# Four adaLN vectors of layer 0: two re-laid on the host, two summed by column groups on TensorE

## The chip, the cores and the metric

The program runs on one core of a Trainium2 chip. The metric is the device time of one execution in microseconds (us), as the median of repeated runs. The engines are written as in the profile: PE (TensorE matmul), PEld (its weight loads), DVE (VectorE), ACT (ScalarE), POOL (GpSimd), SP (SyncE, which here issues nearly all DMAs). A die, a state or a second core play no part.

## What is computed

Two layers of a trunk: layer 0 mixes 1024 latent and 256 context tokens by windowed attention, layer 1 by gated linear attention; a squared-ReLU MLP follows each. Every sub-layer is modulated by vectors that come from `c` (latent) or `c_ctx` (context) through a map of 1024 by 6144 per layer. What the change touches is the first lines of this:

```python
c_lat = jax.nn.silu(c)
c_con = jax.nn.silu(c_ctx)
for i in range(DEPTH):
    m_lat = jnp.split((c_lat @ w_mod[i] + b_mod[i])[:, None, :], N_MOD, axis=-1)
    m_ctx = jnp.split(c_con @ w_mod[i] + b_mod[i], N_MOD, axis=-1)
    h_lat = modulate(x_lat, g_pre_mix[i], m_lat[0], m_lat[1])   # rms_norm * (1 + scale) + shift
    ...
    f_lat = channel_mlp(modulate(x_lat, g_pre_mlp[i], m_lat[3], m_lat[4]), w_mlp_in[i], w_mlp_out[i])
```

Of the six vectors of a layer, 0 and 1 are the mixer's shift and scale, 2 its gate, 3 and 4 the MLP's shift and scale, 5 its gate. All data is float32.

## The kernel before

Tokens are worked on in ten tiles of 128: tiles 0 and 1 are context, 2 to 9 latent. Matrix products with weights are made from pairs of rounded parts, high and low, in three matmuls (`mm3`, lines 226 to 231: `ah`/`al` are the parts of activations, `wqh`/`wql` and `wkvh`/`wkvl` those of the attention weights); `split` (line 212) makes the parts, one copy on ACT and one subtraction on DVE. One tile's q, k and v take 72 matmuls of 512 columns: for each of eight k-slices of the 1024 features, six for q into a two-bank PSUM tile (tag `s`, two of them) and three for k and v into a one-bank tile (tag `b`, four of them).

`first_tiles` (line 523) does tiles 0 and 1 together while the weights arrive, in an order written out by hand (`manual_schedule`, line 1598). Vectors 0 and 1 of layer 0 are made feature tile by feature tile inside it by the three functions of `mod_first` (line 364): `load(c)` fetches the 128 columns of feature tile c of both vectors for all 1024 rows of `w_mod`, as two tiles `wm` of 128 partitions by 8 by 128 numbers; `step(c)` makes 32 matmuls of 128 columns in four column groups of the PE array (two vectors by two halves of the k-slices) with the two columns of `cT` (silu of `c` and `c_ctx`) and copies the result out of PSUM on ACT; `turn(c)` transposes it and makes the columns of `G` (scale times gain) and `S` (shift) on DVE. `operand(k)` applies them to the already turned rows `xT` and splits the result into `ah` and `al`. The loop at line 552 runs, for each k: `step(k+1)`, the weights of k+1 (loads on SP, splits on ACT and DVE), `load(k+2)`, tile 0's product of slice k, `turn(k+1)` and `operand(k+1)`, tile 1's product of slice k. The engines take their instructions in this order; SP too, so a load stands behind the loads ahead of it.

Everything after `first_tiles` is put in order by the framework's planner, which simulates the engines and may move an instruction ahead of others; it also takes the memory slots. `qkv_tile` (line 569) does one tile i from 2 to 9, and calls `between(k)` behind each k-slice; `pre(i+1)` ahead of it normalises, turns (`xt`, two one-bank tiles) and modulates the next tile. The line 1605 makes the generator `mod_sums` (line 288) for vectors 2, 3 and 4 of layer 0, and line 1614 calls it 25 times over the tiles: for each vector and each of the eight row blocks of `w_mod` one load of 512 KB, and for each of the two streams (latent, context) one DVE instruction of 128 by 1024 that multiplies the block by a column of `cT` and adds it up (lines 309 and 311). After the eighth block, `mod_gate` (line 343) sums a gate over the partitions with four matmuls by ones (line 356), and `mod_columns` (line 321) does the same for a shift or scale by 16 transposes (line 332) and four reductions on DVE (line 333). Attention begins after tile 9 (`scores`, line 693: products on PE at 703 to 708, row minimum on DVE at 719). The MLP's shift and scale are read only after attention.

Of the kernel before, what the change touches and what calls it, by code (L numbers as in the profile page):

```python
# [14 lines left out]
ALU = mybir.AluOpType  # L15
# [3 lines left out]
P = 128  # L19
D = 1024  # L20
KT = D // P
# [4 lines left out]
NT = NC_T + NL_T  # L26
# [124 lines left out]
class Weights:  # L151
# [5 lines left out]
    def load(self, n=1):  # L157
        for _ in range(min(n, KT - len(self.got))):
            self.got.append(self.one(len(self.got)))
# [6 lines left out]
class Backbone:  # L166
# [121 lines left out]
    def mod_sums(self, vectors, apart=False):  # L288
# [29 lines left out]
                self.mod_gate(l, j // 3, acc) if j % 3 == 2 else self.mod_columns(l, j, acc)  # L318
        yield

    def mod_columns(self, l, j, acc):

        nc = self.nc
        which = j // 3
        out = self.const([P, 2, KT], f"{'SG'[j % 3]}{l}{which}")
        for s, a in enumerate(acc):
            col = out[:, s, :]
            for q in range(2):
                pt = self.bank("modT")
                for c in range(4):  # L330
                    kk = 4 * q + c
                    nc.tensor.transpose(pt[:, P * c : P * (c + 1)], a[:, P * kk : P * (kk + 1)], self.ident)
                nc.vector.tensor_reduce(
                    out=col[:, 4 * q : 4 * (q + 1)], in_=pt.rearrange("p (c k) -> p c k", c=4), op=ALU.add,
                    axis=mybir.AxisListType.X,
                )
            nc.vector.tensor_tensor(col, col, self.bcol[:, l, KT * j : KT * (j + 1)], op=ALU.add)
            if j % 3 == 1:
                c0 = 16 * which + 8 * l
                nc.vector.scalar_tensor_tensor(col, col, 1.0, self.cols[:, c0 : c0 + KT], ALU.add, ALU.mult)  # L340
        self.pre.setdefault((l, which), [None, None])[1 - j % 3] = out
# [22 lines left out]
    def mod_first(self):  # L364

        nc = self.nc
        G, S = (self.const([P, 2, KT], f"{n}00") for n in "GS")
        self.pre[0, 0] = G, S
        b1 = self.const([P, KT], "b1")
        nc.vector.tensor_scalar(b1, self.bcol[:, 0, 8:16], 1.0, None, ALU.add)  # L370
        w = self.t["w_mod"][0].rearrange("(k p) n -> p k n", p=P)

        def load(c):
            wm = [self.u((P, KT, P), s="wm") for _ in range(2)]
            for j in range(2):
                nc.sync.dma_start(wm[j], w[:, :, D * j + P * c : D * j + P * (c + 1)])
            return wm

        def step(c, wm):
            ps = self.ps1("mod")  # L380
            for k in range(KT):
                for j in range(2):
                    r = 64 * j + 32 * (k % 2)
                    nc.tensor.matmul(
                        ps[r : r + 32, :P], self.cT[:, 2 * k : 2 * k + 32], wm[j][:, k, :],
                        start=(k < 2), stop=(k >= KT - 2), tile_position=(0, r),
                    )
            m = self.half("mod")[:, :P]
            nc.scalar.copy(m, ps[:, :P])
            return m  # L390

        def turn(c, m):
            pc = self.ps1("modT")[:, :P]
            nc.tensor.transpose(pc, m, self.ident)
            even = self.small(4, "even")
            nc.vector.tensor_copy(even, pc.rearrange("p (j d r) -> p j d r", j=2, d=2)[:, :, 0, 0:2])
            nc.vector.scalar_tensor_tensor(
                G[:, :, c], pc[:, 96:98], b1[:, c : c + 1], even[:, 2:4], ALU.add, ALU.add
            )
            nc.vector.tensor_scalar(G[:, :, c], G[:, :, c], self.cols[:, c : c + 1], None, ALU.mult)  # L400
            nc.vector.scalar_tensor_tensor(
                S[:, :, c], pc[:, 32:34], self.bcol[:, 0, c : c + 1], even[:, 0:2], ALU.add, ALU.add
            )

        return load, step, turn
# [117 lines left out]
    def first_tiles(self, xs, h, pre):  # L523

        nc = self.nc
        load, step, turn = self.mod_first()
        self.wq, self.wkv = [], []
        wm = [load(0)]
        xT = [self.u((P, 4, 2 * P), s="xT") for _ in range(2)]
        junk = h.alloc(0)[0][0]  # L530
        xn = [self.normed(xs.pop(0), junk) for _ in range(2)]
        m = step(0, wm[0])
        for q in range(2):
            for i in range(2):
                pt = self.ps1("xt")
                for k in range(4):
                    kk = 4 * q + k
                    nc.tensor.transpose(pt[:, P * k : P * (k + 1)], xn[i][:, P * kk : P * (kk + 1)], self.ident)
                nc.scalar.copy(xT[q][:, :, P * i : P * (i + 1)], pt.rearrange("p (k t) -> p k t", k=4))
        pq, pkv = [self.ps2("q") for _ in range(2)], [self.ps1("kv") for _ in range(2)]  # L540
        G, S = self.pre[0, 0]

        def operand(k):
            t = self.half("h")[:, : 2 * P]
            nc.vector.tensor_scalar(t, xT[k // 4][:, k % 4, :], G[:, 1, k : k + 1], S[:, 1, k : k + 1], ALU.mult, ALU.add)
            self.split(t, *h.group(0, k))

        turn(0, m)
        operand(0)
        self.qkv_weights(0)  # L550
        wm.append(load(1))
        for k in range(KT):
            if k + 1 < KT:
                m = step(k + 1, wm[k + 1])
                self.qkv_weights(k + 1)
            if k + 2 < KT:
                wm.append(load(k + 2))
            self.qkv_mm(h, 0, k, pq[0], pkv[0])
            if k + 1 < KT:
                turn(k + 1, m)  # L560
                operand(k + 1)
            else:
                nxt = pre(2)
            if k == KT - 3:
                xs += [self.x_in(2), self.x_in(3)]
            self.qkv_mm(h, 1, k, pq[1], pkv[1])
        return pq, pkv, nxt
# [1011 lines left out]
    def run(self):  # L1579
        nc, t = self.nc, self.t  # L1580
# [21 lines left out]
        self.attn_consts()  # L1602
        for i in range(2):
            self.qkv_out(i, pq[i], pkv[i])
        mods = self.mod_sums([(0, 2), (0, 3), (0, 4)])
        for i in range(2, NT):
            nxt = pre(i + 1) if i + 1 < NT else None
            if i == NT - 2:
                self.kc = [self.u((P, KVH, CTX), F32R, s="kc") for _ in range(2)]
                self.qs = {}  # L1610
                for f in self.keys(0) + self.keys(1) + self.queries(self.qs, 0, 0):
                    f()
            at = (0, 2, 4, 6) if i == NT - 2 else (0, 2, 5)
            self.qkv_tile(i, h, lambda k: next(mods) if k in at else None)
            h = nxt
            if i < NT - 2:
                self.rotary(i)
# [307 lines left out]
def rope_tables():  # L1925
# [6 lines left out]
    return np.ascontiguousarray(tab.reshape(2, NL_T, P, 32).transpose(2, 0, 1, 3))  # L1932


_INS = [
    "x", "c", "ctx", "c_ctx", "w_mod", "b_mod", "g_pre_mix", "g_post_mix", "g_pre_mlp", "g_post_mlp",
    "w_mlp_in", "w_mlp_out", "attn_w_qkv", "attn_w_o", "attn_sink", "gla_w_in", "gla_w_gate_down",
# [20 lines left out]
```

## Time and profile before

| | us |
|---|---|
| runs (three) | 2611.51, 2612.23, 2617.31 |
| median | 2612.23 |
| the profiled execution | 2614.6 |
| its span, first to last instruction | 2612.5 |
| PE busy in the span | 2547.7 (98%) |
| DVE, ACT, POOL busy | 1718.6, 1259.4, 421.6 |

The span has these stretches around the change: tiles 0 and 1 with vectors 0 and 1 until about 69 us; tiles 2 to 9 with vectors 2 to 4 until about 221 us; then attention, the MLP of layer 0 and layer 1. Busy time counts overlapping instructions once, and a matmul's end is modelled, so neighbouring matmuls overlap in the timeline and their starts tell the pace. "Idle before" in brackets is the time in which the engine had nothing running before the instruction, with what ended it. PEclk is the granted clock of PE as a share of full speed; it goes between two levels, so a mean between them says which share of the stretch was at the lower one. The DMA share is the mean over 16 queues' engines, and goes over 1 where packets overlap.

### The profile page before, as it was taken

The page shows a single profiled execution, that of the slowest core. Times are in us where ns is not written, and L with a number is a line of the kernel's source. Part 1 is how long each engine was busy: PE and PEld are TensorE (multiplying, and loading weights), DVE is VectorE, ACT ScalarE, POOL GpSimd, SP SyncE. Part 2 cuts the span into 40 slices and gives each one's busy share as a digit, 9 for nine tenths or more (in the row PEclk, how much of TensorE's full clock was granted, in tenths as well). Part 3 has the DMA queues.
Part 4 walks back from the last instruction along what each step waited for, and adds up shares of the span by engine and source line. Part 5 has one row for each costly group of instructions (what it writes and reads, how often), then busy time and mean ns, then how long its engine had stood idle before and what let it go on. Part 6 is the DMA issues. An engine that isn't in the chain of part 4 may idle for free.

```text
span 2612.5 us, 36352 instructions
## 1 busy us (share of the span) xinstructions
PE 2547.7 (98%) x13523; PEld 2118.3 (81%) x13523; DVE 1718.6 (66%) x2663; ACT 1259.4 (48%) x2364; POOL 421.6 (16%) x736
## 2 busy tenths in 40 slices
PE   7998999999999999999999999999998999999998
PEld 5777888888888888788877888888887888878886
DVE  4798766756866665758768725736658656566676
ACT  3325777744544444434325635334446545445333
POOL 0354755511000000000002212212310000000001
PEclk9999999999999999999999999999999999999999
DMA  9221000222354565827245331002221554577464
GB/s 311 79 83 41 4 1 18 74 89 81 125 172 145 182 211 188 292 98 268 93 145 193 138 82 60 26 24 97 97 97 49 174 164 133 174 247 236 161 226 161
DMA packets 228129, 342.33 MB, mean 131 GB/s; under 512 B 24409, under 2 KB 122993, under 8 KB 227953
## 3 DMA queue, kind: packets, MB, share of 16 engines
q1 hardware_dynamic: 225360, 330.58, 39.0%
q0 software_dynamic: 2592, 9.44, 0.9%
q8 instruction: 106, 1.74, 0.3%
q14 instruction: 71, 0.57, 0.1%
HBM read 267.60 MB, written 72.35 MB: 130 GB/s over the span
## 4 chain that ended last, share of the span: by engine, by line
PE 84%; DVE 7%; DMA 4%; issue 2%; ACT 2%; POOL 1%; SPq 0%; DVEq 0%; POOLq 0%; ACTq 0%
PE p L229 7%; PE p L231 6%; PE p L230 6%; PE pa L230 4%; PE pa L229 4%; PE pa L231 4%; PE o L771 3%; PE pt L752 3%; PE y L231 3%; PE y L229 3%; PE y L230 3%; PE rp L230 2%; PE rp L229 2%; PE rp L231 2%; PE pc L229 2%
## 5 line engine op out<-in xcount | busy, mean ns | idle before, releaser
L230 PE MATMUL p<-ol,oh 128*128 128x512 f32 x896 | 350.0, 391 | 0.1
L231 PE MATMUL p<-oh,ol 128*128 128x512 f32 x896 | 346.2, 389 | 0.0
L229 PE MATMUL p<-oh 128*128 128x512 f32 x896 | 329.7, 392 | 6.0 <-ACT oh L213 4.8
L242 POOL TENSOR_SCALAR rs<-ss 128x1 f32<-128x1 f32 (+1 forms) x78 | 27.6, 353 | 1636.3 <-ACT later L236 1452.2
L214 DVE TENSOR_TENSOR ol<-wh,oh 128x1024 fp32r<-128x1024 f32 x128 | 153.6, 1222 | 94.9 <-ACT oh L213 94.4
L229 PEld LDWEIGHTS p<-oh 128*128 128x128 f32 x896 | 168.3, 188 | 45.3 <-ACT oh L213 6.4
L230 PEld LDWEIGHTS p<-ol,oh 128*128 128x128 f32 x896 | 168.5, 188 | 36.4 <-DVE ol L214 1.0
L231 PEld LDWEIGHTS p<-oh,ol 128*128 128x128 f32 x896 | 168.5, 188 | 35.2 <-issue 0.2
L213 ACT CAST oh<-wh 128x1024 fp32r<-128x1024 f32 x128 | 131.4, 1051 | 131.2 <-DVE wh L1114 28.8
L311 DVE SCALAR_TENSOR_TENSOR ma<-wm,cT,ma 128x1024 f32<-128x1024 f32 x112 | 149.0, 1362 | 51.5 <-DMA wm<-in_w_mod 51.5
L213 ACT CAST oh<-k 128x1024 fp32r<-128x1024 f32 x96 | 98.0, 1054 | 127.6 <-PE p L231 57.0
L214 DVE TENSOR_TENSOR wi<-wi,wi 128x512 fp32r<-128x512 f32 x176 | 116.6, 687 | 47.9 <-ACT wi L213 46.2
L944 ACT COPY s<-pa 128x512 f32<-128x512 f32 x96 | 56.1, 585 | 182.3 <-PE pa L231 178.3
L719 DVE CUSTOM_DVE_ANT_0 pr<-sc,mask,nsink 128x640 f32<-128x640 f32 (+2 forms) x144 | 108.5, 775 | 41.8 <-PE sc L708 39.9
L724 ACT ACTIVATE pr<-pr,nm 128x640 f32<-128x640 f32 (+2 forms) x160 | 118.6, 742 | 27.3 <-DVE nm L719 24.2
L214 DVE TENSOR_TENSOR ol<-k,oh 128x1024 fp32r<-128x1024 f32 x96 | 113.8, 1221 | 21.3 <-ACT oh L213 17.7
L736 POOL TENSOR_SCALAR pr<-pr,den 128x640 f32<-128x640 f32 (+2 forms) x160 | 118.1, 752 | 36.3 <-DVE den L734 16.5
L213 ACT CAST wi<-wi 128x512 fp32r<-128x512 f32 x176 | 103.6, 615 | 38.7 <-DMA hd<-h 24.1
L229 PE MATMUL y<-woh,oh 128*128 128x512 f32 x288 | 113.9, 396 | 0.0
L231 PE MATMUL y<-woh,ol 128*128 128x512 f32 x288 | 112.5, 391 | 0.9 <-DVE ol L214 0.9
L230 PE MATMUL y<-wol,oh 128*128 128x512 f32 x288 | 112.3, 390 | 0.0
L231 PE MATMUL rp<-wgh,al 128*128 128x512 f32 x288 | 112.1, 390 | 0.0
(379 smaller groups left out, 6746.0 us busy)
## 6 DMA issues: line engine op xcount, KB each, us to landing
wm<-in_w_mod SPq DMA_DIRECT2D x96, 512.0 KB, 4.6
hd<-h SPq DMA_DIRECT2D x80, 512.0 KB, 2.9
wh<-hd SPq DMA_DIRECT2D x144, 256.0 KB, 3.9
wh<-in_w_mlp_out SPq DMA_DIRECT2D x144, 256.0 KB, 4.3
wi<-in_w_mlp_in SPq DMA_DIRECT2D x64, 512.0 KB, 5.1
k<-hd SPq DMA_DIRECT2D x80, 256.0 KB, 5.3
k<-in_w_mlp_out SPq DMA_DIRECT2D x80, 256.0 KB, 5.4
x<-in_x SPq DMA_DIRECT2D x16, 512.0 KB, 3.5
```

The lines of the kernel that those rows point to most:

```text
L213: self.nc.scalar.copy(hi, src)
L214: self.nc.vector.tensor_tensor(lo, src, hi.bitcast(F32), op=ALU.subtract)
L229: mm(out, a[0], b[0], start=start, stop=False, skip_group_check=onto)
L230: mm(out, a[0], b[1], start=False, stop=False, skip_group_check=onto)
L231: mm(out, a[1], b[0], start=False, stop=stop, skip_group_check=onto)
L311: nc.vector.scalar_tensor_tensor(acc[s], raw, c, acc[s], ALU.mult, ALU.add)
L719: nc.vector.tensor_tensor_reduce(out=like(pr), in0=like(ps[e][:, off:768]), in1=mask, scale=1.0, scalar=self.nsink[:, c0 + e : c0 + e + 1] ...
L724: nc.scalar.activation(pr, pr, AF.Exp, bias=nm[:, e : e + 1], scale=-1.0, accum_out=sums[:, e : e + 1])
L736: nc.gpsimd.tensor_scalar(probs[e], probs[e], den[:, e : e + 1], 0.0, ALU.mult, ALU.add)
L752: nc.tensor.transpose(pt[:, P * j : P * (j + 1)], probs[e][:, P * kt : P * (kt + 1)], self.ident)
L771: nc.tensor.matmul(po[64 * e : 64 * (e + 1), P * i4 : P * (i4 + 1)], self.kv[tile_i // 2][:, tile_i % 2, 256 + HD * g : 256 + HD * (g + 1) ...
L944: nc.scalar.copy(s["s", j], s["pa"])
```

## The change

The first part adds an input, `first`: the host cuts columns 0 to 2047 of layer 0's `w_mod` into [feature tile, vector, partition, k-slice by column], so that each `wm` tile of `mod_first` is one contiguous block with 4 KB for each partition. What is loaded into the tile is the same.

The second part moves, for k = 0 alone, tile 0's product ahead of `step(1)` and the weights of k = 1.

The third part takes vectors 3 and 4 out of `mod_sums` and makes them in a new generator `mod_pair`: per row block two loads (the blocks of both vectors, in flight two row blocks at a time), and four matmuls with 32 columns of `cT` as weights (the first two are the streams) and 512 columns of a block, one in each column group of the array, all eight row blocks summed in one PSUM bank. One ACT copy, four transposes into a second bank, and small DVE instructions then give the columns. Its six steps are called in tiles 5 to 8; vector 2 keeps `mod_sums`, in tiles 2 to 4.

```diff
+    def mod_pair(self, l, which):
+        nc, t = self.nc, self.t
+        js = (3 * which, 3 * which + 1)
+        def load(k):
+            raw = [self.u(s="wm") for _ in js]
+            for r, j in zip(raw, js):
+                nc.sync.dma_start(r, t["w_mod"][l, P * k : P * (k + 1), D * j : D * (j + 1)])
+            return raw
+        raws = [load(0), load(1)]
+        yield
+        ps = self.ps1("mod")
+        for k in range(0, KT, 2):
+            for kk in (k, k + 1):
+                raw = raws.pop(0)
+                for b in range(4):
+                    nc.tensor.matmul(
+                        ps[32 * b : 32 * (b + 1), :], self.cT[:, 2 * kk : 2 * kk + 32],
+                        raw[b // 2][:, 512 * (b % 2) : 512 * (b % 2 + 1)],
+                        start=(kk == 0), stop=(kk == KT - 1), tile_position=(0, 32 * b),
+                    )
+            if k + 2 < KT:
+                raws += [load(k + 2), load(k + 3)]
+            else:
+                m = self.half("mod")
+                nc.scalar.copy(m, ps)
+            yield
+        pt = self.ps1("modT")
+        for c in range(4):
+            nc.tensor.transpose(pt[:, P * c : P * (c + 1)], m[:, P * c : P * (c + 1)], self.ident)
...
+            for st in range(2):
+                nc.vector.tensor_tensor(...)            # plus bias, 8 columns
+                if v == 1:
+                    nc.vector.scalar_tensor_tensor(...) # (scale + 1) * gain, 8 columns
...
-        w = self.t["w_mod"][0].rearrange("(k p) n -> p k n", p=P)
+        w = self.t["first"]
...
-                nc.sync.dma_start(wm[j], w[:, :, D * j + P * c : D * j + P * (c + 1)])
+                nc.sync.dma_start(wm[j], w[c, j].rearrange("p (k n) -> p k n", k=KT))
...
         for k in range(KT):
+            if k == 0:
+                self.qkv_mm(h, 0, k, pq[0], pkv[0])
             if k + 1 < KT:
                 m = step(k + 1, wm[k + 1])
                 self.qkv_weights(k + 1)
             if k + 2 < KT:
                 wm.append(load(k + 2))
-            self.qkv_mm(h, 0, k, pq[0], pkv[0])
+            if k > 0:
+                self.qkv_mm(h, 0, k, pq[0], pkv[0])
...
-        mods = self.mod_sums([(0, 2), (0, 3), (0, 4)])
+        mods, pair = self.mod_sums([(0, 2)]), self.mod_pair(0, 1)
...
-            at = (0, 2, 4, 6) if i == NT - 2 else (0, 2, 5)
-            self.qkv_tile(i, h, lambda k: next(mods) if k in at else None)
+            def between(k):
+                if i < 5 and k in (0, 2, 5):
+                    next(mods)
+                elif (i, k) in ((5, 5), (6, 1), (6, 5), (7, 1), (7, 5), (8, 1)):
+                    next(pair)
+            self.qkv_tile(i, h, between)
...
+def first_columns(w_mod):
+    w = w_mod[0, :, : 2 * D].reshape(KT, P, 2, KT, P)
+    return np.ascontiguousarray(w.transpose(3, 2, 1, 0, 4).reshape(KT, 2, P, KT * P))
```

## Rows read from the trace of the kernel before

**Rows 1.** Busy time by stretch, columns: length, each engine, PEclk, DMA share, GB/s.
```profile
70.00:224.00 154.00, 148.69 (x696) 121.27 (x696) 124.11 (x151) 45.51 (x87) 63.53 (x62) 0.99 0.27 86
190.00:200.00 10.00, 5.76 (x29) 5.08 (x28) 7.18 (x10) 3.29 (x8) 6.46 (x8) 0.83 0.00 0
224.00:2612.00 2388.00, 2345.05 (x12394) 1956.35 (x12392) 1561.94 (x2439) 1187.20 (x2234) 353.65 (x652) 1.00 0.40 129
```

**Rows 2.** The DMA view: packets of 20 to 45 us, then of 55 to 62.
```profile
DMA packets 10530, 8.14 MB, mean 326 GB/s; under 512 B 245, under 2 KB 9443, under 8 KB 10527
...
DMA packets 788, 2.87 MB, mean 410 GB/s; under 512 B 88, under 2 KB 88, under 8 KB 788
```

**Rows 3.** Timeline of the first stage: start, duration, engine, line, instruction, count.
```profile
10.54 1.93 PE L384 MATMUL mod<-wm,cT 128*32 128x128 f32 x30 [1.06 <-DMA wm<-in_w_mod]
...
22.72 0.48 PE L229 MATMUL q<-wqh,ah 128*128 128x512 f32 x1
...
26.11 0.27 ACT L389 COPY mod<-mod 128x128 f32<-128x128 f32 x1 [1.41 <-PE mod L384]
```

**Rows 4.** Timeline, the tail of the first stage, SP's issues among it.
```profile
45.40 4.15 SPq L479 DMA_DIRECT2D x<-in_x  x2
...
49.64 0.38 SPq L221 DMA_DIRECT2D wqr<-in_attn_w_qkv  x1
...
54.29 1.07 PE L384 MATMUL mod<-wm,cT 128*32 128x128 f32 x30 [1.54 <-DMA wm<-in_w_mod]
...
58.12 1.05 ACT L213 CAST wqh<-wqr 128x1024 fp32r<-128x1024 f32 x1 [2.35 <-DMA wqr<-in_attn_w_qkv]
...
62.08 0.66 PE L229 MATMUL q<-wqh,ah 128*128 128x512 f32 x1 [2.25 <-ACT ah L213]
...
64.03 0.75 DVE L427 TENSOR_SCALAR x<-x,rs 128x1024 f32<-128x1024 f32 x1 [1.54 <-POOL rs L243]
...
68.32 0.39 PE L230 MATMUL kv<-wkvl,ah 128*128 128x512 f32 x1
...
68.54 0.39 PE L231 MATMUL kv<-wkvh,al 128*128 128x512 f32 x1
```

**Rows 5.** Waits of SP, 0 to 70 us: total, times, longest.
```profile
SPq L479 <- DVE al L214: 8.1, 2, 6.3
```

**Rows 6.** Loads of line 221 (attention weights, 512 KB each), issue to landing.
```profile
DMA to landing us min/median/max: 5.6/7.2/8.4
```

**Rows 7.** Groups of instructions, 62 to 226 us: busy, mean ns, idle before.
```profile
L311 DVE SCALAR_TENSOR_TENSOR ma<-wm,cT,ma 128x1024 f32<-128x1024 f32 x42 | 61.0, 1498 | 7.1 <-DMA wm<-in_w_mod 7.1
...
L332 PE MATMUL modT<-ident,ma 128*128 128x128 f32 x32 | 4.3, 273 | 0.5 <-DVE ma L311 0.5
```

**Rows 8.** Timeline of PE: a step of 32 matmuls, and one of mod_gate's fours.
```profile
24.96 1.08 PE L384 MATMUL mod<-wm,cT 128*32 128x128 f32 x32
...
129.54 0.39 PE L230 MATMUL q<-wql,ah 128*128 128x512 f32 x1
129.85 1.05 PE L356 MATMUL mod<-ma,ones 128*32 128x512 f32 x4
...
131.17 0.39 PE L229 MATMUL q<-wqh,ah 128*128 128x512 f32 x1
```

**Rows 9.** Timeline ahead of tile 9's transposes, DVE and PE.
```profile
190.60 3.63 DVE L311 SCALAR_TENSOR_TENSOR ma<-wm,cT,ma 128x1024 f32<-128x1024 f32 x2
194.16 0.89 DVE L427 TENSOR_SCALAR x<-x,rs 128x1024 f32<-128x1024 f32 x1
...
195.20 1.79 PE L439 MATMUL xt<-ident,x 128*128 128x128 f32 x8 [4.24 <-DVE x L427]
...
199.00 0.48 PE L229 MATMUL kv<-wkvh,ah 128*128 128x512 f32 x1
```

**Rows 10.** Timeline at the start of attention, PE and DVE.
```profile
220.87 0.40 PE L708 MATMUL sc<-kc,qs 128*128 128x256 f32 x2
...
224.62 0.48 DVE L719 CUSTOM_DVE_ANT_0 pr<-sc,mask,nsink 128x256 f32<-128x256 f32 x1
```

More of the change, by code (lines that the diff above doesn't have):

```diff
@@ L319, in mod_sums @@
         yield
+    def mod_pair(self, l, which):
[27 more added lines that the diff above has]
+            nc.tensor.transpose(pt[:, P * c : P * (c + 1)], m[:, P * c : P * (c + 1)], self.ident)
+        p5 = pt.rearrange("p (c v h r) -> p v r h c", c=4, v=2, h=2)
+        out = []
+        for v, j in enumerate(js):
+            col = self.const([P, 2, KT], f"{'SG'[v]}{l}{which}")
+            for st in range(2):
+                nc.vector.tensor_tensor(
+                    col[:, st, :].rearrange("p (h c) -> p h c", h=2), p5[:, v, st],
+                    self.bcol[:, l, KT * j : KT * (j + 1)].rearrange("p (h c) -> p h c", h=2), op=ALU.add,
+                )
+                if v == 1:
+                    c0 = 16 * which + 8 * l
+                    nc.vector.scalar_tensor_tensor(
+                        col[:, st, :], col[:, st, :], 1.0, self.cols[:, c0 : c0 + KT], ALU.add, ALU.mult
+                    )
+            out.append(col)
+        self.pre[l, which] = out[::-1]
+        yield
     def mod_columns(self, l, j, acc):
@@ L1948 @@
     arrays["in_rope"] = rope_tables()
+    arrays["in_first"] = first_columns(inputs["w_mod"])
     t = {
```

## The prediction

> **What bounds the kernel now.** I read four views in this order. The busy time by stretches [rows 1] splits the program: from 224 us on PE is busy for 2345 of 2388 us at full granted clock, and nothing that the change edits runs there; the change lives in the first 224 us. Between 70 and 224 us (the projections of tiles 2 to 9) PE is busy for 148.7 of 154 us, with DVE second at 124.1. So in that stretch any PE instruction added is paid for, and DVE work taken away is worth only the places where PE stood still for DVE. I looked for those in the timeline of PE and found one large one, 4.24 us before 195.20 [rows 9].
>
> The first 62 us are different: two things take turns. In the middle PE is continuously busy; at the ends it waits for data. The DMA view [rows 2] shows the queues full: 326 GB/s while `w_mod` and `w_qkv` loads are mixed, 410 GB/s later, when 788 packets carry 2.87 MB (mean 3.6 KB). In the mixed stretch 9443 of 10530 packets are below 2 KB. The issues on SP are held up too: two loads of `x` take 4.15 us to issue at 45.40 [rows 4].
>
> **Part 1: the layout of the first two vectors.** It removes no bytes. Sixteen loads of 512 KB, each in 1024 rows of 512 bytes, become 16 loads in 128 rows of 4 KB. From the two rates one gets the rate of short rows: `wm` is 8.4 of the 14.7 MB that are loaded in this mix, 57%, so 1/326 = 0.57/r + 0.43/410, r = 282 GB/s. At 410 the 8.4 MB of `wm` cost 20.5 us of DMA time, not 29.8. What the stage needs before its last product, about 17 MB, takes 41.5 us at that rate from 2 us on, while PE comes to the last step of the vectors at 52: the queue stops being full.
>
> The Trainium skill speaks against this gain (DMA: Bandwidth & Descriptors, Specifications): it gives 512 bytes as the size from which a transfer reaches line rate, so rows of 512 bytes would lose nothing. The trace has 326 against 410 GB/s, which does not agree; by the rule the term below is zero, and that is rival B.
>
> Where it counts is the tail of the stage. Before: step(7) of the vectors waited 1.54 us for `wm`; the last `wqr` was issued at 49.64, behind the two `x` loads, and landed at 58.1, where ACT waited 2.35 us for it; from that cast to the first product of the last k is 3.96 us (58.12 to 62.08); PE had stood 2.25 us and came back at the lower clock (that product lasts 0.66 us, those at the end 0.39); the stage's last product started at 68.54, 0.22 after the one before it, so the next could have started at 68.77 [rows 4]. After: the two `x` loads still wait on SP for DVE (the waits of SP name `al` L214 [rows 5], about 47.2), then cost 0.4 each to issue, as `wqr` itself did (0.38), so `wqr` goes out at 48.0. With the queue drained I take the shortest landing of its line, 5.6 us [rows 6]: 53.6. PE leaves step(7) 1.54 earlier, at 53.7, runs nine products at 0.23 each and the turn, 55.9; what follows the turn on DVE and ACT is at most 3.96 less the cast's 1.05, and I take 2.0, so the last k starts at the later of 53.6 + 3.96 and 55.9 + 2.0 = 57.9, without the low clock. Its nine products end at 60.0. Tile 2's normalised rows come 2.7 us after that start (64.78 against 62.08), at 60.6, then eight transposes and nine products, 3.0: 63.6 against 68.8. **Term: -5.2.** Bounds: 0 if the last load stays late, -6.6 if the wait for the normalised rows vanishes too. That the next tile then waits 1.4 us for ACT is as before.
>
> **Part 2: the first product goes ahead of step(1).** Nine PE instructions pass 32 others on PE's queue; no DMA, no other engine. Before, the product stood behind step(1) and its data; the second tile's began at 22.72 [rows 3]. Now it needs only the splits of the first weights on ACT and DVE, and these end up behind step(0): its data came at 10.54, after 1.06 us in which PE waited behind its first two small products, so all may come up to 1.6 us sooner. But PE is then still at the lower clock, where nine products take nearly twice as long (0.66 against 0.39 each, [rows 4]), and step(1) and its turn follow one on the other, so that the turn waits for ACT's copy of 0.27 [rows 3] with its two handovers, 0.45, which the product used to cover. I end within 0.2 us of 22.72. **Term: 0**, between -1.6 and +1.2.
>
> **Part 3: layer 0's MLP shift and scale.** It removes, on DVE, 28 of the 42 accumulations L311, two thirds of 61.0 us [rows 7], their four first products and eight reductions: some 49 us of DVE; on PE 32 transposes L332, half of which lie before 220.87. It adds, on PE, 32 matmuls of 32 weights by 512 float32 columns, in four bursts of eight, and four transposes; one ACT copy of 128x512 and six DVE instructions on 8 columns, hidden: ACT is busy 45.5 of 154 us and DVE has just been relieved [rows 1]. The loads on SP are the same 16, now four at a time in tiles 5 to 7; behind them stand `x` loads wanted about two tiles later, and four loads at 410 GB/s are 5 us. A burst is not in the trace, but its neighbours are [rows 8]: behind the product at 129.54, four such matmuls (`mod_gate`) push the second next product from 130.00 to 131.17, 1.17 us; 32 matmuls of 128 columns, the same column count as eight of 512, run in 1.08. So a burst of eight lies between 1.2 and 2 x 1.17 = 2.3; a straight line from four (each further one 0.15) gives 1.8. I take 1.5, nearer the row with the same columns. Four bursts +6.0, four transposes +0.45. The 16 transposes removed took 2.2 us of PE by their group (4.3 us for 32) and half a microsecond of waiting for L311 [rows 7]; I take 2.5. The stall: DVE starts L427 of the last tile at 194.16 because L311 occupies it until then, PE starts the transposes at 195.20 after 4.24 idle, and 20 transposes take until 199.00, in a slice with 0.83 of the clock granted [rows 1], where 20 x 0.11 would do (half of their busy time at the low clock, eight in 1.79): 4.2 + 1.5 = 5.7 [rows 9]. Without L311 DVE has nothing ahead of L427 from about 190 on, before PE runs out. **Term: -2.5 + 6.45 - 5.7 = -1.7**, between -3.4 and +4.3 (bursts at 2.3 and only half of the stall gone).
>
> At the start of attention, DVE first ends the vector of the scale behind the other 16 transposes, and it reads the first scores only at 224.62, though they have been there since 221.3 [rows 10]. **Term: -3.0**, between -1.6 (the transposes alone) and -3.3.
>
> **Sum.** -5.2 + 0 - 1.7 - 3.0 = -9.9 us. The profiled execution took 2614.6 (span 2612.5 and 2.1 around it), so it would be 2604.7; it was 2.4 above the median of the runs, 2612.2, which gives **2602.3**.
>
> **Rivals.** **B, the layout gains nothing:** the tail is held by SP's wait for DVE and by slots, or short rows cost no rate. For it: SP's wait for `al` [rows 5]; against it: 326 and 410 GB/s. Then -1.7 - 3.0: 2607.5. **C, PE pays and DVE's relief is not collected:** bursts split into fours by the order on PE cost 2.3 each, and the stall at 191 to 195 goes to another cause (POOL's chain for the same factors). -5.2 - 2.5 + 9.4 + 0.45 - 1.6 = +0.6: 2612.8. Against it: DVE ran L311 up to the very start of L427. **D, slower: PSUM banks.** The accumulator `mod` holds one of the four one-bank tiles from tile 6 into tile 7 and `modT` one in tile 8; `xt` takes two, `kv` one. If a `kv` product finds no bank, PE stands until the modulation of `xt` has drained, about 5 us a tile with the return at the lower clock (as at 195 to 199); over three tiles +15, so +5.1: 2617.3. It decides once `kv` of a tile comes up before its predecessor's copy; against it, 48 `q` products (11 us) stand between.
>
> **How the numbers follow.** Forecast 0.62 (its own range 2597 to 2607), B 0.12, C 0.14, D 0.08, others, above all another order of the instructions after 224 us, 0.04. The range 2595 to 2613 takes in the forecast's bounds, B and C, and leaves D out. A measurement of this kernel tells some 0.2% (5.2 us) from no change: faster than 2607 is nearly all of the forecast and part of B, 0.68; within, 0.23; slower, 0.09.
>
> **What would show it.** Right: over 400 GB/s and no full queue in the first 50 us; the first stage's last product near 63; four bursts of about 1.5 us; no PE gap over 1 us before the last transposes `xt`; the first score row read within 1 us of its scores. Wrong: a gap at `wqr` in the tail (B), bursts of 2 us or more or the gap at `xt` still there (C), waits of PE for `kv` or `xt` banks in tiles 6 to 8 (D).

## The result, and the profile after

The changed kernel took 2620.67 us (median of 9 runs, 2617.90 to 2625.24), the kernel before 2613.76 (median of 9, 2610.83 to 2617.33): ratio 1.0023, 95% interval 1.0014 to 1.0032. It is slower by 6 to 7 us where 9.9 us less were forecast, and it lies above the range of 2595 to 2613. The profiled execution took 2621.45 us, with a span of 2619.7.

Busy time by stretch, after (columns as in [rows 1]):

```profile
20.00:30.00 10.00, 9.24 (x89) 6.77 (x90) 4.09 (x9) 3.20 (x6) 0.00 (x0) 0.86 1.03 402
...
70.00:224.00 154.00, 154.00 (x704) 113.57 (x703) 81.54 (x113) 42.63 (x81) 53.61 (x62) 1.00 0.25 83
```

DVE is relieved as forecast: 81.5 us between 70 and 224 where it had 124.1 [rows 1]. PE no longer pauses there at all (154.00 of 154, 148.69 before) and yet ends later: it has more to do. The DMA view of 20 to 45 us, after, answers [rows 2]:

```profile
DMA packets 3155, 10.12 MB, mean 405 GB/s; under 512 B 307, under 2 KB 307, under 8 KB 3152
```

The layout does what was expected of it: a third of the packets and 405 GB/s for 326. The mix with rows of 512 bytes moved a fifth less than the one without them. The Trainium skill (DMA: Bandwidth & Descriptors, Specifications) has transfers at line rate from 512 bytes on. The trace does not agree, and the measurement decides. The last `wqr` is no longer held on SP until 49.64 [rows 4]:

```profile
38.64 0.33 SPq L221 DMA_DIRECT2D wqr<-in_attn_w_qkv  x1
```

The groups of instructions between 70 and 224 us, after (columns as in [rows 7]):

```profile
L340 PE MATMUL mod<-wm,cT 128*32 128x512 f32 x64 | 14.6, 603 | 0.0
...
L408 PE MATMUL mod<-ma,ones 128*32 128x512 f32 x8 | 2.1, 605 | 0.0
```

L340 is the new matmul. The source issues it 32 times, and the profile has 64 records; `mod_gate` (L408) issues 4 and has 8. So it is with the steps of the first two vectors: `step` issues 16 matmuls (eight k-slices by two vectors) and not the 32 of the section on the kernel before, which is the count of records. The new matmuls keep PE busy for 14.6 us where the prediction has 6.0. The timeline of PE shows how they stand, after:

```profile
150.46 1.92 PE L340 MATMUL mod<-wm,cT 128*32 128x512 f32 x16
152.31 0.51 PE L229 MATMUL kv<-wkvh,ah 128*128 128x512 f32 x1
...
159.74 0.39 PE L231 MATMUL q<-wqh,al 128*128 128x512 f32 x1
160.06 1.05 PE L340 MATMUL mod<-wm,cT 128*32 128x512 f32 x4
161.04 0.50 PE L229 MATMUL q<-wqh,ah 128*128 128x512 f32 x1
161.38 0.39 PE L230 MATMUL q<-wql,ah 128*128 128x512 f32 x1
```

One group of 16 records passes in 1.85 us (2.1 with its edges). The other 48 come as twelve fours, each between two products: two matmuls, which use two of the four column groups. A four moves the second next product from 160.20 (0.23 apart, twice, after 159.74) to 161.38, 1.2 us, as the fours of [rows 8] did. That makes 2.1 + 12 x 1.17 = 16 us.

The start of the first stage, PE's timeline, after:

```profile
18.60 0.51 PE L229 MATMUL q<-wqh,ah 128*128 128x512 f32 x1 [2.80 <-ACT wqh L213]
19.86 0.80 PE L230 MATMUL q<-wql,ah 128*128 128x512 f32 x1 [0.75 <-DVE wql L214]
20.45 0.63 PE L231 MATMUL q<-wqh,al 128*128 128x512 f32 x1
20.88 0.63 PE L229 MATMUL q<-wqh,ah 128*128 128x512 f32 x1
...
23.20 1.08 PE L436 MATMUL mod<-wm,cT 128*32 128x128 f32 x32
24.66 0.33 PE L446 MATMUL modT<-ident,mod 128*128 128x128 f32 x1 [0.39 <-ACT mod L441]
24.75 0.48 PE L229 MATMUL q<-wqh,ah 128*128 128x512 f32 x1
...
60.20 0.48 PE L229 MATMUL q<-wqh,ah 128*128 128x512 f32 x1
...
67.57 0.50 PE L229 MATMUL q<-wqh,ah 128*128 128x512 f32 x1 [1.39 <-ACT q L635]
```

Before, the first product stood behind `step(1)`, with nothing between them:

```profile
19.85 0.79 PE L229 MATMUL q<-wqh,ah 128*128 128x512 f32 x1
```

The second tile's first product is at 24.75 (22.72 before, [rows 3]); the stage's last k starts at 60.20 without the waits of [rows 4]; tile 2 starts at 67.57 (70.35 before).

Where the time went, by the start of the same matmul in both traces, after less before:

| stretch | forecast | measured | shift at its end |
|---|---|---|---|
| to the second tile's first product | 0 | +2.0 | +2.0 |
| from there to tile 2 | -5.2 | -4.8 | -2.8 |
| tiles 2 to 9, to 220 us | -1.7 | +7.5 | +4.7 |
| start of attention, to 275 us | -3.0 | -0.3 | +4.4 |
| 275 us to the end | 0 | +2.9 | +7.3 |

### The profile page after: what moved, and what is told of

Read it like the earlier page. It is cut to its first block, busy times and chain, and to the rows that moved or that the text cites. A ratio compares the mean times of both kernels' runs of the same rounds, so it can differ in the third digit from the quotient of the medians.

```text
span 2619.7 us, 36383 instructions
## 1 busy us (share of the span) xinstructions
PE 2560.9 (98%) x13559; PEld 2116.6 (81%) x13559; DVE 1674.8 (64%) x2623; ACT 1260.6 (48%) x2365; POOL 412.8 (16%) x736
## 4 chain that ended last, share of the span: by engine, by line
PE 85%; DMA 5%; DVE 4%; issue 2%; ACT 2%; POOL 1%; SPq 1%; DVEq 0%; POOLq 0%; ACTq 0%
PE p L230 6%; PE p L229 6%; PE p L231 6%; PE pa L230 4%; PE pa L231 4%; PE pa L229 4%; PE o L826 4%; PE pt L807 3%; PE y L231 3%; PE y L229 2%; PE y L230 2%; PE rp L229 2%; PE rp L230 2%; PE rp L231 2%; PE pc L229 2%; PE pc L231 2%
## 5 line engine op out<-in xcount | busy, mean ns | idle before, releaser
L311 DVE SCALAR_TENSOR_TENSOR ma<-wm,cT,ma 128x1024 f32<-128x1024 f32 x84 | 108.8, 1322 | 46.9 <-DMA wm<-in_w_mod 46.9
L230 PE MATMUL rp<-wgl,ah 128*128 128x512 f32 x288 | 112.3, 390 | 0.0
```

Of the source, the lines that this page charges most:

```text
L230: mm(out, a[0], b[1], start=False, stop=False, skip_group_check=onto)
L311: nc.vector.scalar_tensor_tensor(acc[s], raw, c, acc[s], ALU.mult, ALU.add)
```

## The experiments

Two theories stood against each other for each half. For the column groups: they cost about 16 us of PE because a float32 matmul is two passes and most of them run as fours (passes), or they cost 6 and the loss is an effect of where they stand (place). For the first stage: the move costs what the layout gains (move), or the layout gains less than the profile says (layout). The first runs do one or two parts alone. Edits are against the changed kernel where nothing else is said, and `...` marks what is left out.

**Layout alone.**

```diff
-            if k == 0:
-                self.qkv_mm(h, 0, k, pq[0], pkv[0])
...
+            self.qkv_mm(h, 0, k, pq[0], pkv[0])
...
-        mods, pair = self.mod_sums([(0, 2)]), self.mod_pair(0, 1)
+        mods = self.mod_sums([(0, 2), (0, 3), (0, 4)])
...
```

> The kernel before with the new layout of vectors 0 and 1 alone; the order of the first loop and the sums of vectors 3 and 4 on DVE are as before. Theory (the order of the first product costs 2.4 us at the start, the layout gives 5.3 at the tail): tile 2 starts 5.2 us earlier than before (at 65.1 instead of 70.35, where the changed kernel has 67.57), and some 5 us are left at the end, 2608 to 2609. Rival (the start is late in the changed kernel because of the layout itself, as the loads now come in another rhythm): tile 2 at 67.6 as in the changed kernel, 2611.

2609.89 us, ratio 0.9987 (0.9977 to 0.9996): faster by some 3.4 us. PE's timeline:

```profile
17.31 1.07 PE L436 MATMUL mod<-wm,cT 128*32 128x128 f32 x30 [0.81 <-DMA wm<-in_first]
18.31 0.50 PE L229 MATMUL q<-wqh,ah 128*128 128x512 f32 x1
...
20.52 0.47 PE L229 MATMUL q<-wqh,ah 128*128 128x512 f32 x1
...
62.92 0.50 PE L229 MATMUL q<-wqh,ah 128*128 128x512 f32 x1 [1.39 <-ACT q L632]
...
189.11 1.30 PE L491 MATMUL xt<-ident,x 128*128 128x128 f32 x5 [4.22 <-DVE x L479]
```

With `step(1)` in its old place PE is at work until the split weights are there (18.31), at the full clock, and the second tile follows at 20.52. Tile 2 starts 7.4 us earlier than before, 2.2 of it at the start, which was not expected, and 5.2 behind it. The stall at tile 9's transposes is still there: 4.22.

**Layout and move.**

```diff
-        mods, pair = self.mod_sums([(0, 2)]), self.mod_pair(0, 1)
+        mods = self.mod_sums([(0, 2), (0, 3), (0, 4)])
...
```

> Layout and the order of the first product together, vectors 3 and 4 on DVE as before. Theory: tile 2 at 67.6 as in the changed kernel, 2.8 us earlier than before, and the stall of 4.2 us before the last transposes is back; 2610 to 2612 at the end. Rival (the stall at the last transposes depends on when tile 2 begins): stall gone, -7 us.

2614.76 us, ratio 1.0004 (0.9994 to 1.0013). The second tile's first product is at 25.49, tile 2 at 68.32: the move takes back 5.4 of the 7.4 us, and nothing of it is won later.

**Column groups alone**, old layout and old order.

```diff
-        w = self.t["first"]
+        w = self.t["w_mod"][0].rearrange("(k p) n -> p k n", p=P)
...
-            if k == 0:
-                self.qkv_mm(h, 0, k, pq[0], pkv[0])
...
```

> The kernel before with vectors 3 and 4 on TensorE alone; old layout, old order. Theory (each float32 matmul is two passes on PE, and they run in fours of 0.98 us plus 0.17 at the edges, twelve of them and one run of sixteen, 16 us; 5.7 us of the stall and 2.5 of transposes come back): level with before until 145 us, +7.5 at the start of attention, 2619 to 2622. Rival (the loss in the changed kernel comes from PSUM banks or from loads that the faster first stage shifts): under +3 us.

2619.36 us, ratio 1.0019 (1.0009 to 1.0028): slower by themselves. Between 145 and 217 us the shift against before goes from -2.6 to +5.0, 7.6 us, as in the changed kernel (-2.9 to +4.7).

**The kernel before once more**, because in the last run the first stage, whose code is that of before, reached tile 2 by 67.82.

> The kernel before, unchanged, looked at once more. The one-pair experiment had the first stage of before word for word, but its tile 2 began at 67.82 us and not at 70.35. If this is the spread of the first stage from one execution to the next, tile 2's first product begins anywhere from 67.5 to 70.5 here and the waits behind the last w_mod tile and the last weights differ from the profile of before by 1 to 2 us each; the rival is that the planner placed the pair kernel's loads otherwise: then this run repeats 70.3 within 0.3 us. Time 2611 to 2617 either way.

2611.37 us. PE's timeline in the tail of the first stage:

```profile
61.02 0.50 PE L229 MATMUL q<-wqh,ah 128*128 128x512 f32 x1 [2.27 <-ACT ah L213]
...
68.41 0.50 PE L229 MATMUL q<-wqh,ah 128*128 128x512 f32 x1 [1.40 <-ACT q L580]
```

The same program reaches tile 2 in 68.41 here and in 70.35 in the profile on which the prediction rests. From the second tile's first product to tile 2 it takes 45.1 (23.27 to 68.41) and not 47.6; with the new layout it takes 42.4 (layout alone) and 42.8 (layout and move, and the changed kernel). With column groups alone, whose first stage is that of before, it took 44.6. So the tail is worth 1.7 to 5.2 us, not always 5.

**The move alone**, old layout, no column groups; here the edit is against the kernel before.

```diff
+            if k == 0:
+                self.qkv_mm(h, 0, k, pq[0], pkv[0])
...
+            if k > 0:
+                self.qkv_mm(h, 0, k, pq[0], pkv[0])
-            self.qkv_mm(h, 0, k, pq[0], pkv[0])
```

> The kernel before with the move alone: first product ahead of step(1), old layout, no column groups. The prediction had this at 0 (-1.6 to +1.2) and named the lower clock and the copy of 0.45 us as its price. With the new layout it cost 4.9 us, and beside the column groups 7. If the price is TensorE's idle stretch while the weights are split (2.8 us) and step(1) on the path behind it, it is there with the old layout too, at least in part, since step(1) had to wait for its loads until 17.99 anyway: second tile's first product at 24.5 to 26 instead of 22.72 and 2616 to 2618 us. If it is an effect of the new layout's order of loads alone, 22.7 within 0.5 and 2612 to 2615.

2615.97 us, ratio 1.0006 (0.9997 to 1.0016). The second tile's first product is at 26.74, 4 us late, but tile 2 is at 69.56, where the old first stage had 67.82, 68.41 and 70.35 without the move: 42.8 us from one to the other. The start is as the first theory has it, and later still than its 24.5 to 26; the time lies just below its 2616 to 2618 and within the noise of before. With the old layout the loads end the stage, and most of PE's late start hides behind them. With the new one PE ends it, and the late start is paid.

**No move**: layout and column groups.

```diff
-            if k == 0:
-                self.qkv_mm(h, 0, k, pq[0], pkv[0])
...
```

> The changed kernel with the first product back behind step(1); layout and column groups stay. Theory: the move costs some 5 us in the first stage, whatever stands behind it, so tile 2 begins at 62.9 (67.57 in the changed kernel), the ten tiles end with some 4.5 us less than in the changed kernel, and the time is about 2616 us (2614.5 to 2617.5), still above before by 1 to 3 us because the column groups cost some 16 us of TensorE against the 8.2 that they save. Rival: the later tiles wait for loads anyway and give the start back; then the time stays at 2619 to 2621.

2613.27 us, ratio 1.0003 (0.9994 to 1.0013); the median is 7.4 below that of the changed kernel, more than the 5 expected, and 5.2 by the ratios (0.0020 of 2613). Its profiled execution (2620.71) was the slowest of its ten runs. Even so its second tile is at 23.47 and tile 2 at 65.85, ahead of the four traces with the new layout and the move as it is (24.65 to 25.51, and 67.52 to 68.37).

The six combinations against before, by their ratios, in us: layout -3.4, move +1.6, column groups +5.0, layout and move +1.0, layout and groups +0.8, all three +6.0; each within 2.5. Layout and groups add up within that; the move adds 4.4 to 5.2 wherever the layout is new, and 1.6 with the old one, a difference that the times alone do not show beyond their noise.

**Half of the column groups.** The matmuls of the odd row blocks (the "odd feature tiles" of the expectation) are left out, with all loads kept; the vectors that come of it are wrong.

```diff
-                for b in range(4):
+                for b in range(4) if kk % 2 == 0 else ():
...
-                        start=(kk == 0), stop=(kk == KT - 1), tile_position=(0, 32 * b),
+                        start=(kk == 0), stop=(kk == KT - 2), tile_position=(0, 32 * b),
```

> The changed kernel with the matmuls of the odd feature tiles left out of layer 0's MLP shift and scale (every load stays), so that 16 of the 32 matmuls are gone. Theory: each float32 matmul is two passes on TensorE and the 64 passes cost 16 us where they stand; half of them gone brings 7 to 8 us, the records at that line halve from 64 to 32, and the time is 2612.5 to 2614. Rival, the price of the prediction (6.0 us for all): 3 us less, 2617 to 2618. Second rival: what costs is the place of the bursts in the order and not their length; then less than 2 us.

2613.63 us, 7.0 below the changed kernel. The group of the new matmuls, 70 to 224 us:

```profile
L340 PE MATMUL mod<-wm,cT 128*32 128x512 f32 x32 | 7.4, 605 | 0.0
```

16 matmuls fewer are 32 records and 7.2 us of PE less, and at 217 us the same matmuls start 7.2 us earlier than in the changed kernel (shift against before -2.5, and +4.7). The forecast's price (3 us for this half) is out, and so is the place.

**Whole bursts.** Loads two steps further ahead, the groups in tiles 2 to 5, the remaining sum on DVE in tiles 5 to 7.

```diff
-        raws = [load(0), load(1)]
+        raws = [load(k) for k in range(4)]
-                if i < 5 and k in (0, 2, 5):
+                if 5 <= i < 8 and k in (0, 2, 5):
...
-                elif (i, k) in ((5, 5), (6, 1), (6, 5), (7, 1), (7, 5), (8, 1)):
+                elif (i, k) in ((2, 1), (3, 3), (3, 6), (4, 2), (4, 6), (5, 1)):
```

> The changed kernel with the loads of vectors 3 and 4 two steps ahead, in tiles 2 to 5 (vector 2 then in tiles 5 to 7), so that the matmuls stand on PE in four unbroken runs of eight, all four column groups one after the other, instead of pairs with products between. Theory (a run of two column groups leaves half of the array idle): each run of sixteen passes takes 1.9 us and 0.3 at its edges, 8.6 in all and not 16: 7 us less than the changed kernel at the start of attention, 2612 to 2614. Rival (passes cost 0.245 us each however they stand): 2620 as the changed kernel.

2619.68 us, ratio 1.002 (1.0011 to 1.003): no gain, against 2612 to 2614 expected. It is the time of the rival, but not for its reason. The group of the new matmuls, 97 to 128 us:

```profile
L340 PE MATMUL mod<-wm,cT 128*32 128x512 f32 x64 | 7.7, 598 | 0.0
```

PE's timeline, where the gain went:

```profile
158.37 0.88 PE L491 MATMUL xt<-ident,x 128*128 128x128 f32 x6 [1.86 <-DVE x L479]
...
177.78 1.09 PE L491 MATMUL xt<-ident,x 128*128 128x128 f32 x8 [1.96 <-DVE x L479]
```

The 64 records take 7.7 us instead of 14.6 when they come in sixteens. But the sum that went to tiles 5 to 7 now stands ahead of two normalisations, as that of tile 8 did before, and PE waits 1.86 and 1.96 us for them. At 217 us the shift is +0.6 (changed kernel +4.7), so 4.1 us of the gain are left. It goes to -1.7 at 225 and is back at +3.3 by 275: the rest is lost at the start of attention, where PE has 0.50 of the clock from 230 to 235 us (more on this below).

**DVE's sums dealt out otherwise**; the edit is against layout alone.

```diff
...
-            at = (0, 2, 4, 6) if i == NT - 2 else (0, 2, 5)
+            at = {2: (0, 2, 4, 6), 3: (0, 2, 4, 6), 4: (0, 2, 4, 6), 8: (), 9: (0, 2, 4, 6)}.get(i, (0, 2, 5))
```

> Layout alone, no column groups; the 25 steps of the vector engine's sums are dealt out otherwise: four in each of tiles 2 to 4 (three before), none in tile 8 (four before), four in tile 9. Theory: the wait of 4.2 us before the last tile's transposes is there only because two steps of the sums stand ahead of its normalisation on the vector engine, which idles for some 18 us between 60 and 120 us; it goes without any work being taken off that engine, and the time is 2604 to 2606. Rival: the vector engine is full up to there and the wait only moves to an earlier tile (a gap of 2 us or more before another xt or q): 2608 to 2611.

2611.53 us, ratio 0.9994 (0.9985 to 1.0004): the theory fell. PE's timeline at its waits:

```profile
137.92 0.80 PE L229 MATMUL q<-wqh,ah 128*128 128x512 f32 x1 [2.22 <-ACT ah L213]
...
170.75 1.06 PE L491 MATMUL xt<-ident,x 128*128 128x128 f32 x8 [0.95 <-DVE x L479]
...
191.81 1.42 PE L659 MATMUL kt<-ident,k 128*128 128x128 f32 x6 [2.77 <-POOL k L654]
```

The stall of 4.2 is gone and comes back as three others, 5.9 together. With three vectors on it DVE is busy for 93 to 100% of every 10 us from 90 to 190; its relief is worth something, as the prediction had it.

**Clock or order.** Why does the move cost 4 to 5 us? In the changed kernel a repeat of `step(0)`, which nobody reads, was put ahead of the first product, once and then three times.

```diff
             if k == 0:
+                again = self.ps1("mod")
+                for n in range(3 * KT):        # KT in the first of the two
+                    kk = n % KT
+                    for j in range(2):
+                        r = 64 * j + 32 * (kk % 2)
+                        nc.tensor.matmul(again[r : r + 32, :P], self.cT[:, 2 * kk : 2 * kk + 32], wm[0][j][:, kk, :], ...)
                 self.qkv_mm(h, 0, k, pq[0], pkv[0])
```

> The changed kernel with one thing added: a second run of step(0)'s 16 matmuls, whose result nobody reads, stands ahead of the first product, where step(1) stood before. It takes no data that is not there; it fills the 2.8 us in which TensorE otherwise waits for the split weights. Two theories of why the move costs 4 to 5 us. Clock: TensorE idles, so its products run at the lower clock (0.43 us apart, 0.23 at the full one); then nine products win some 1.8 us, and the second tile's first product comes at 23.0 us or before (24.75 without the filler, 20.52 with layout alone). Order: step(1) and its turn no longer lie in the wait for the splits but behind the product, so that 1.1 us of matmuls and two waits of 0.4 us for ACT are on the path; then the second tile's product is at 24.5 or later. I expect both: about 23.2, and a granted clock near 1.00 from 18 to 30 us.

With one repeat, 2622.57 us, a miss: it ended at 16.4, PE still waited 1.79 us, the products were still 0.43 us apart, and the second tile came at 25.63, later than the 24.75 without it. The run could not tell the two apart. PE's row of the stretch (length, busy, granted clock, DMA share, GB/s):

```profile
20.00:30.00 10.00, 9.22 (x85) 0.74 1.03 404
```

> The changed kernel with three runs of step(0)'s matmuls ahead of the first product instead of the one of the filler before: 3.2 us of matmuls from 15.4 us on, so that TensorE works until the split weights are there at 18.3 to 18.6 us. One run ended at 16.4 and left 1.79 us idle and the clock low (0.60 to 0.74), so it could not tell clock from order. Now the clock theory gives products 0.23 us apart from the start: the first nine end near 21.2 and step(1) takes 1.08; the second tile's first product comes at 22.8 to 23.3 (24.75 in the changed kernel, 25.63 with one filler), and the rest against 20.52 is order. If the products are still 0.43 us apart, or the second tile is not before 24.3, the clock is not what the idle stretch decides here. The times of the whole kernel differ by too little for one look: 2616 to 2622.

With three, 2617.68 us. The timeline of PE:

```profile
15.53 2.85 PE L611 MATMUL mod<-wm,cT 128*32 128x128 f32 x96
18.41 0.50 PE L229 MATMUL q<-wqh,ah 128*128 128x512 f32 x1
19.67 0.50 PE L230 MATMUL q<-wql,ah 128*128 128x512 f32 x1 [0.76 <-DVE wql L214]
20.00 0.39 PE L231 MATMUL q<-wqh,al 128*128 128x512 f32 x1
20.23 0.39 PE L229 MATMUL q<-wqh,ah 128*128 128x512 f32 x1
...
21.71 1.08 PE L436 MATMUL mod<-wm,cT 128*32 128x128 f32 x32
23.17 0.33 PE L446 MATMUL modT<-ident,mod 128*128 128x128 f32 x1 [0.39 <-ACT mod L441]
23.26 0.47 PE L229 MATMUL q<-wqh,ah 128*128 128x512 f32 x1
...
26.98 0.50 PE L229 MATMUL q<-wqh,ah 128*128 128x512 f32 x1 [0.40 <-ACT ah L213]
```

PE works through the wait, the products come 0.23 us apart, and the second tile starts at 23.26, inside the 22.8 to 23.3 of the expectation. From the first product to the second tile it is 4.85 us here and 6.15 in the changed kernel: 1.3 us are the clock, and tile 2 comes 1.5 earlier (66.12, against 67.57).

For the order, the run with the sums dealt out otherwise is the nearest: its first stage is that of layout alone, with `step(1)` ahead of the product. PE's timeline there:

```profile
18.48 0.50 PE L229 MATMUL q<-wqh,ah 128*128 128x512 f32 x1 [0.43 <-ACT wqh L213]
19.75 0.51 PE L230 MATMUL q<-wql,ah 128*128 128x512 f32 x1 [0.76 <-DVE wql L214]
...
21.70 0.48 PE L229 MATMUL q<-wqh,ah 128*128 128x512 f32 x1
```

The product starts when it does with three repeats, at the same clock and with the same wait for `wql`, and the second tile comes 1.6 us sooner (21.70 for 23.26). That is order: `step(1)` now lies behind the product instead of in the wait for the splits (1.0, 21.71 to 22.7), PE waits for ACT's copy (0.39), and the rest is the joints between them. The last 1.2 us, to the 20.52 of layout alone, are not the move's: that execution alone had no wait for `wql`. In the four traces with the new layout and without the move the second tile is at 20.52, 21.14, 21.70 and 23.47, in the last of them with the products 0.43 us apart behind 0.89 us of idle PE; in the four with the move and without repeats it is at 24.65 to 25.51. The groups do not overlap, and their means are 3.4 us apart at the second tile and 3.8 at tile 2.

**A version from these parts**: new layout, no move, whole bursts, and the nine steps left on DVE dealt one or two a tile.

```diff
-        raws = [load(0), load(1)]
+        raws = [load(k) for k in range(4)]
...
-            if k == 0:
-                self.qkv_mm(h, 0, k, pq[0], pkv[0])
...
-                if i < 5 and k in (0, 2, 5):
+                if k in {4: (5,), 5: (2, 5), 6: (2, 5), 7: (2, 5), 8: (5,), 9: (2,)}.get(i, ()):
...
-                elif (i, k) in ((5, 5), (6, 1), (6, 5), (7, 1), (7, 5), (8, 1)):
+                elif (i, k) in ((2, 1), (3, 3), (3, 6), (4, 2), (4, 6), (5, 1)):
```

> A version meant to be faster than both: new layout, first product behind step(1) as before, the pair's loads four feature tiles ahead in tiles 2 to 5 so that its 64 passes run in four unbroken bursts of 16 (1.9 us each), and the 9 steps left to the vector engine dealt one or two a tile over tiles 4 to 9. Against layout alone (2609.9): bursts +8.6 with their edges, transposes -2.5, the wait before the last xt and its low clock -5.7, so about the same or 1 us better at 225 us: 2607 to 2610. If unbroken bursts still cost 16 us by the clock or by banks, 2613 or more; if the wait before xt comes back because sums still stand ahead of a normalisation, 2611 to 2613.

2606.74 us (median of 8, 2602.90 to 2609.32), ratio 0.9974 (0.9964 to 0.9984): 7 us faster than before, and by the ratios some 13 faster than the changed kernel. The timeline of the new matmuls:

```profile
95.50 1.92 PE L340 MATMUL mod<-wm,cT 128*32 128x512 f32 x16
...
119.72 1.92 PE L340 MATMUL mod<-wm,cT 128*32 128x512 f32 x16
```

Busy time by stretch (columns as in [rows 1]):

```profile
62.00:216.00 154.00, 151.80 (x740) 119.40 (x740) 82.11 (x123) 49.98 (x98) 55.08 (x66) 1.00 0.21 72
```

Four sixteens, no wait over 0.5 us between tile 2's start and tile 9's end, and the full clock. The first product waits for nothing but the splits, behind `step(1)`. This is one kernel with three of the parts changed at once; how much each gives was not measured in it.

## Why the prediction was wrong

**Part 1 (tail -5.2): right, with luck in its size.** The mechanism is as told in the main: over 400 GB/s, no wait behind `wm`, no gap at the last k, -4.8 measured and -5.2 with layout alone. One step of it came otherwise. The last `wqr` was to go out at 48.0, behind two held `x` loads, and went out at 38.64; the prediction's sum went by PE's own path (57.9) and not by that load (53.6 + 3.96), so its size did not suffer. And the profile before had a long tail: against its second execution the same new tail is worth 2.3. Layout alone was 7.4 us ahead at tile 2, 4.4 at 275 us (1.3 went to a new wait for ACT at 153.68), and 3.4 by its ratio. Rival B is out.

**Part 2 (0): the step that failed is the cover.** The prediction says that the data "may come up to 1.6 us sooner" and that the lower clock and ACT's copy take this back, within 0.2 us. The product did come 1.25 sooner than before (18.60 for 19.85). But from it to the second tile's first product it was 6.15 us and not 2.87: 0.75 of waiting for `wql`, some 1.0 for the clock, and 1.5 for `step(1)` with ACT's copy behind it. The prediction counts the copy alone (0.45) as what the product used to cover, and neither `step(1)` nor `wql`. `step(1)` had been free, in the wait for the split weights (with layout alone the product starts at 18.31 behind it), and was moved onto the path: +2.0 against before. And the term was worked out on the trace before, where the loads end the stage. There the move is mostly covered by tile 2 (69.56, where the old first stage had 67.82 to 70.35); Part 1 takes this cover away. The two terms were added as if each stood alone.

**Part 3 (-1.7): the mis-sized term is the bursts, 6.0 for 16.** The prediction read "x4" at `mod_gate` [rows 8] as four matmuls, and "x32" at the step as 32; they are two and 16. By the rows read rightly, eight matmuls of 512 columns, with twice the columns of such a step (1.08), take 2.2 in one piece and 4 x 1.17 = 4.7 in fours; the one in one piece took 1.85. The rest of the part came as told: the stall before the last `xt` is gone (5.7), the 16 transposes too (2.5), and 16.1 + 0.45 - 5.7 - 2.5 = +8.4, with +7.5 measured; the other 0.9 is not traced to a place. Rival C had the mechanism (bursts split into fours), at 9.4 for 16. Its other half is out: DVE's relief was collected.

Two records a matmul and, in a sixteen, four records in turn for each column group in 1.85 us make 0.46 a record, twice the 0.23 of a `q` matmul of the same columns. The Trainium skill (FP8 and Floating Point Precision, TensorE Precision Notes) gives four passes for a true float32 product. The trace agrees in effect: 2 x 0.46 is four times 0.23. An estimate from that page, four times 0.23 for each of 32 matmuls, four side by side, is 7.4 us; whole sixteens took 7.7.

**Start of attention (-3.0): won, then given back.** DVE reads the first scores at once, as forecast, and the shift falls from +4.7 to +2.4 at 225 us. Then PE waits 1.23 and 0.67 us, and its clock falls:

```profile
230.00:235.00 5.00, 3.80 (x17) 3.21 (x18) 4.60 (x18) 4.64 (x20) 3.22 (x11) 0.59 0.00 0
235.00:240.00 5.00, 5.00 (x38) 4.03 (x38) 3.16 (x13) 3.48 (x13) 3.15 (x11) 0.73 0.02 3
```

Before, the clock was 1.00 from 225 to 240, through waits no shorter (1.04, 0.63, 1.25). 0.41 and 0.27 of 5 us are at most 3.4 us of full clock, and the shift is back at +4.4. The dip does not belong to the column groups: the move alone, whose program from tile 2 on is that of before, has it too, and its shift goes from -0.5 at 217 us to +1.1 at 240:

```profile
230.00:235.00 5.00, 4.76 (x29) 3.86 (x28) 3.31 (x14) 3.88 (x17) 4.43 (x14) 0.66 0.01 2
```

Each of the twelve traces of a changed program has such a slice of 5 us between 215 and 240, at 0.50 to 0.68 of the clock, the fastest version's too (0.50, and its shift goes from -10.5 at 225 us to -6.1 at 275). Only the two executions of the kernel before are without it. What decides it stays open.

**After 275 us (0, +2.9): open.** It begins behind waits of layer 0's MLP for DVE that differ from run to run: PE's longest wait there was 1.50 before, 2.29 in the changed kernel and 0.81 in the fastest version. From 275 us to the end the other runs moved between -1.2 and +4.3 against the same profile, the second execution of before by -1.2. Whether the column groups have a share in it was not settled.

Rival D, PSUM banks, is out: PE has no wait between 70 and 224 us after.

## What to carry to other kernels

Count the matmuls of the source before taking a duration from a row: a float32 matmul is two records here, so a count on the page is not a count of instructions, and a price per instruction has to be divided by the right one. Cost a part in the kernel that the other parts leave behind: what is hidden while loads end the stage is paid once they don't. Read a start from more than one execution before splitting it into causes: the same first stage began its second tile anywhere from 20.52 to 23.47. Work that lies in a wait costs nothing where it is and everything where it is moved to.

## What the hardware showed that was not expected

- Two float32 matmuls on two column groups take 0.98 us and eight on four groups 1.85: 64 records cost 14.6 us of PE in one sixteen and twelve fours, and 7.7 in four sixteens. Feeding all four groups at once took half the time.
- 1.1 us of added matmuls, followed by 1.79 us of idleness, left the products at the lower clock (1.2 GHz, 0.43 us apart); 2.9 us of them, up to the product, gave the full one (2.4 GHz, 0.23 apart). The granted clock of the whole stretch from 20 to 30 us was 0.74 and 1.00.
- The first stage of one and the same program took 2 us more or less from one execution to the next (70.35 and 68.41), more than several of the prediction's terms.
